# A decoder layer on one core: four modulation rows move into the Strassen pairs, and two small parts of the down projection change places

## The chip, the core and the metric

The kernel runs on one core of one Trainium2 chip. The core has five engines that run side by side: TensorE (PE, matrix products, with its weight loads shown apart as PEld), VectorE (DVE), ScalarE (ACT), GpSimd (POOL) and SyncE (SP, which here only issues transfers). They share an on-chip memory, TensorE writes its results into the accumulator banks PSUM, and 16 DMA engines move data from and to the main memory. ACT and POOL issue transfers too, each on a queue of its own. The metric is the device time of one execution in microseconds, from runs on the chip; lower is better.

## What is computed

One layer of a decoder: a mixer (an mLSTM head group and a convolution group) and a feed-forward part with a causal convolution, each between norms and scaled by a condition vector. The part that matters here is the modulation and the feed-forward:

```python
cond = jax.nn.silu(c)
mod = cond @ ada_w[l] + ada_b[l]
sh1, sc1, g1, sh2, sc2, g2 = jnp.split(mod[:, None, :], N_MOD, axis=-1)
...
u = rms_norm(x, ffn_pre_g[l]) * (1.0 + sc2) + sh2
up = causal_dwconv(u @ ffn_up[l], ffn_conv_w[l], ffn_conv_b[l])
a, gt = jnp.split(up, 2, axis=-1)
f = (jax.nn.silu(gt) * a) @ ffn_down[l]
x = x + g2 * rms_norm(f, ffn_post_g[l])
```

There are 512 positions, 1024 channels and 2816 feed-forward channels, all in float32. The last eighth of `mod` (48 blocks of 128 numbers), `g2`, is used only at the very end.

## The kernel before

**Numbers in two parts.** TensorE multiplies numbers of a shorter format. Each float32 operand z is therefore split into a high part `zh` (ACT copies it into the short format) and a low part `zl` = z - `zh`, and each product is made of three matmuls: high by high, high by low, low by high. The low part comes from VectorE (`split`), from GpSimd (`w_split`), or, in `added_split`, from a transfer: ACT writes -`zh` into `zl` and a DMA issued by POOL adds z to it (line 1088).

**The feed-forward up part.** The 2816 channels are 22 units of 128, each with a value half and a gate half. Units 0 to 7 are plain: two halves of 24 matmuls (512 wide), then `conv3` on ACT and VectorE (names `fa<i>c`, `fg<i>c`; two taps at line 999), a silu on ACT (line 1141) and a product on VectorE into a tile F (line 1142). Units 8 to 21 go in seven pairs, m = 4 to 10: the even unit i by a Strassen scheme of seven half-size products, the odd unit j plainly. TensorE's order in a pair is: four first products (p1, p7, p5, p6), the value half of j, three last products (p2, p3, p4), the gate half of j. The last products add onto banks that VectorE has to combine first (`between`, lines 1113 to 1116; line 1115 writes the bank `upx` that p2 goes on with). So line 1115 must be done when the value half is.

**The order around.** From the first pair on, ACT, VectorE and POOL run in the order in which the code is written (`in_order`); TensorE and SP always do. Before the pairs a scheduler orders ACT, VectorE and POOL, from its estimates and a few order marks.

**The modulation rows.** A row of `mod` is one 128 x 1024 tile of the weights, times the condition vector `cb`, summed on VectorE with one instruction (`ada_block`, line 155, followed by a short read of the accumulator). Rows 40 to 47 are `g2`. Rows 40 to 43 are summed just before the plain units' first results, rows 44 to 47 behind the results of units 4 and 5, marked to stand behind their line 1142. `ada_done` (line 160) and `gain` (line 667) finish them; `send_rows`, in pair m = 9, turns them and sends them to main memory, and in pair m = 10 ACT issues two transfers (line 663) that spread them over all partitions (`g2r`). Tiles `ada` come from a pool of two buffers, which pairs 9 and 10 use for other things.

**The down part.** It is Strassen again, over 11 blocks m of 256 channels. Its first half makes products with the forms b1, t1, t3, t2 of each weight block (`forms1`, `parts1`; b1 of blocks 0 to 4 by `part_b`, that is by `added_split`). The first product of all needs `b_0`, which is made in the last pair, m = 10, behind `g2r`'s transfers on ACT. The second half needs b2, b4 and t4 of each block and the parts of the tiles `g2kept`. `load2` brings for each block the quarter for b2, the quarter for b4 and the stored t2 (`t2_d`), from which `forms2` (line 1245) makes t4's source; `parts2` splits all three. VectorE's steps there carry order marks only ("order on VectorE"). Buffers `wd` and `wdmore` hold the loads, and each is used again for a later block, so a load waits until the splits of the earlier block have read it. At the end, the products of blocks 8 to 10 are taken apart by token blocks: first those with t4 (token blocks 2 and 3), then those with b2 and b4 (blocks 0 and 1), so that the final norm of each can start early. Each is followed on ACT and VectorE by a sum of squares, a factor and the addition of x, and by the transfer of the result.

Of the kernel before, what the change touches and what calls it, by code (L numbers as in the profile page):

```python
# [17 lines left out]
P = 128  # L18
# [34 lines left out]
def decoder_layer(ctx, tc, w_glu0, x, xT, c, adaT, vecs, w_glu, w_qko, w_v0, w_v, w_out, w_up, w_down, out):  # L53
# [1086 lines left out]
    def unit_out(i, a, g, F):  # L1140
        S.activation(g, g, AF.Silu)
        return V.tensor_tensor(out=F[:, (i % 2) * T : (i % 2 + 1) * T], in0=a, in1=g, op=ALU.mult)

# [84 lines left out]
    def load2(m):  # L1228
        r = wd_raw(m + NM, 2)
        loaded[m] = [quarter(r, b) for b in range(3)]  # L1230
        nc.sync.dma_start(r[:, :T], w_down[m][:, :T])
        nc.sync.dma_start(r[:, T : 2 * T], w_down[m][:, 3 * T :])
        nc.sync.dma_start(r[:, 2 * T : 3 * T], t2_d[m])

# [22 lines left out]
    for m in range(MS):  # L1257
        open_F(m)
        for i in (2 * m, 2 * m + 1):
            pa, pg = plain_unit(i)  # L1260
            if m < MS - 1:
                done = unit_out(i, conv3(pa, i, f"fa{i}"), conv3(pg, NF + i, f"fg{i}"), Fs[m])
                if i > 3:
                    for n in (2 * i + 36, 2 * i + 37):
                        ada_block(n, done)
                if i == 5:
                    ada_done(40, 48)
                    gain(3, 40, "ffn_post_g")
            elif i % 2 == 0:
                even = pa, pg  # L1270
            if i in (3, 4):
                token_forms(i - 3)
# [16 lines left out]
    with in_order():  # L1289
# [14 lines left out]
        for m in range(MS, NM):  # L1304
# [12 lines left out]
            bg = conv3(bg, NF + bj, f"fg{bj}")  # L1317
            weight_form(i, "p3", s4)
            if more_to_come:
                for n, q in ((i, 2), (i, 0), (j, 0), (i, 3), (j, 1), (i, 1)):  # L1320
                    up_load(n + 2, (q,))
# [24 lines left out]
            else:  # L1346
                part_b(0)
                part_b(1)
# [6 lines left out]
            if more_to_come:  # L1355
                weight_form(i + 2, "p7", a11)
                weight_form(i + 2, "p5", a21)
                value = [value_part(j + 2, 0)]
                V.tensor_tensor(out=a11, in0=a22, in1=a11, op=ALU.subtract)
            if m - 1 < SPILLED:  # L1360
# [7 lines left out]
            if more_to_come:  # L1368
                weight_form(i + 2, "p6", a11)
                value.append(value_part(j + 2, 1))  # L1370
            unit_out(i, vx, vz, Fs[m])
            before = j, va, pg
        more = upool.tile([P, 2, 2048], F32, tag="uh", name="wdmore")
# [87 lines left out]
    for m in range(NM):  # L1461
# [3 lines left out]
        if m > 1:  # L1465
            forms2(m)
            w2[m] = parts2(m)
        if M2 - NT <= m < M2:
# [139 lines left out]
```

## Time and profile before

| | |
|---|---|
| runs on the chip | 775.94, 772.1 and 770.09 us, median 772.1 |
| the profiled execution | 770.89 us, its span 769.2 us |
| TensorE clock granted | 0.999 |
| ACT busy | 449.0 us of the span (58%) |
| DMA | 148.47 MB, on the mean 193 GB/s |

The span runs from the first to the last instruction of the profiled execution; the time of that execution is 1.7 us longer. All moments below are microseconds from the span's start.

Busy time of the engines in stretches of 20 us (the last one 29) tells where in the program what is full:

```profile
440.00:460.00 20.00, 20.00 (x136) 18.54 (x135) 17.15 (x22) 11.71 (x20) 8.05 (x8) 1.00 0.86 223
...
500.00:520.00 20.00, 18.64 (x108) 16.15 (x108) 18.07 (x34) 14.15 (x26) 9.85 (x9) 1.00 0.77 196
...
580.00:600.00 20.00, 20.00 (x129) 18.27 (x128) 14.52 (x24) 13.53 (x25) 11.24 (x10) 1.00 0.74 174
...
640.00:660.00 20.00, 18.59 (x99) 15.79 (x98) 16.31 (x28) 12.23 (x23) 4.41 (x5) 1.00 0.94 267
...
720.00:740.00 20.00, 20.00 (x90) 16.57 (x89) 20.00 (x36) 13.75 (x28) 0.00 (x0) 1.00 0.86 291
740.00:769.00 29.00, 22.07 (x96) 17.58 (x95) 20.23 (x36) 10.20 (x24) 2.21 (x4) 0.97 0.44 162
```

Each row has the stretch, its length and then the busy time of TensorE, its weight loads, VectorE, ACT and GpSimd with the number of instructions, and last the granted clock, the share of time that the DMA engines were busy, and GB/s. The plain units run from about 440 to 506, the pairs from 506 to 655, the down part from there. TensorE is full nearly everywhere: it misses 1.4 us in the row of the first pair, 1.4 in the row in which the down part begins, and 6.9 in the last, which holds the final additions. VectorE is nearly full before the pairs, has some 5 us free in 20 within them, and is full again in the down part.

### The profile page before, as it was taken

The page shows a single profiled execution, that of the slowest core. Times are in us where ns is not written, and L with a number is a line of the kernel's source. Part 1 is how long each engine was busy: PE and PEld are TensorE (multiplying, and loading weights), DVE is VectorE, ACT ScalarE, POOL GpSimd, SP SyncE. Part 2 cuts the span into 40 slices and gives each one's busy share as a digit, 9 for nine tenths or more (in the row PEclk, how much of TensorE's full clock was granted, in tenths as well). Part 3 has the DMA queues.
Part 4 walks back from the last instruction along what each step waited for, and adds up shares of the span by engine and source line. Part 5 has one row for each costly group of instructions (what it writes and reads, how often), then busy time and mean ns, then how long its engine had stood idle before and what let it go on. Part 6 is the DMA issues. An engine that isn't in the chain of part 4 may idle for free.

```text
span 769.2 us, 11554 instructions
## 1 busy us (share of the span) xinstructions
PE 754.2 (98%) x3961; PEld 644.7 (84%) x3961; DVE 641.4 (83%) x1034; ACT 449.0 (58%) x860; POOL 367.6 (48%) x320
## 2 busy tenths in 40 slices
PE   7999999999999999999999999999999999999996
PEld 6888898778888888988888998878999989788884
DVE  6978999999999966756858789888877766999996
ACT  5457266776666447572353556677667656556752
POOL 1029587696798645442761444446665553100001
PEclk9999999999999999999999999999999999999999
DMA  9983214213022452425952788879877788799882
GB/s 331 380 291 137 84 55 164 82 51 143 29 90 102 161 172 106 165 109 182 373 202 109 248 221 220 247 191 275 202 179 174 177 239 202 219 338 373 288 301 109
DMA packets 55999, 148.47 MB, mean 193 GB/s; under 512 B 6370, under 2 KB 7810, under 8 KB 51844
## 3 DMA queue, kind: packets, MB, share of 16 engines
q1 hardware_dynamic: 33588, 100.37, 37.6%
q10 hardware_dynamic: 14288, 32.68, 12.1%
q0 software_dynamic: 8064, 14.68, 11.0%
q8 instruction: 31, 0.51, 0.3%
q14 instruction: 28, 0.23, 0.1%
HBM read 117.42 MB, written 15.61 MB: 173 GB/s over the span
## 4 chain that ended last, share of the span: by engine, by line
PE 59%; DVE 27%; DMA 5%; ACT 4%; issue 3%; ACTq 1%; POOL 0%; DVEq 0%; SPq 0%; POOLq 0%
DVE cv L731 10%; PE up L189 4%; PE up L190 4%; PE up L188 4%; PE upx L1095 4%; PE glu L316 3%; PE glu L189 3%; PE glu L190 3%; PE glu L188 3%; PE p L189 3%; PE p L190 3%; PE p L188 3%; PE mixa L188 2%; PE mixa L190 2%; PE mixa L189 2%
## 5 line engine op out<-in xcount | busy, mean ns | idle before, releaser
L731 DVE SCALAR_TENSOR_TENSOR cv<-gt,cvw,cv 128x505 f32<-128x505 f32 (+24 forms) x200 | 137.2, 729 | 2.3 <-ACT cv L719 1.1
L727 POOL TENSOR_TENSOR cs<-cs,cs 128x510 f32<-128x510 f32 (+3 forms) x32 | 41.8, 1305 | 0.3
L685 POOL TENSOR_TENSOR ro2r<-ro2t,mhalf 128x1 f32<-128x1 f32 x1 | 0.6, 559 | 81.3 <-DVE ro2t L683 81.3
L155 DVE SCALAR_TENSOR_TENSOR junk<-ada,cb 128x1024 bf16<-128x1024 f32 x20 | 31.2, 1562 | 7.9 <-DMA ada<-in_adaT 7.7
L725 ACT ACTIVATE cs<-gt,cvw 128x511 f32<-128x511 f32 (+4 forms) x40 | 27.4, 716 | 6.1 <-POOL cs L727 2.8
L188 PE MATMUL up<-u2h,wup_0h 128*128 128x512 f32 (+1 forms) x72 | 25.7, 357 | 0.2 <-DVE fa7c L999 0.2
L189 PE MATMUL up<-u2l,wup_0h 128*128 128x512 f32 (+1 forms) x72 | 25.7, 356 | 0.2 <-DVE u2l L910 0.2
L190 PE MATMUL up<-u2h,wup_0l 128*128 128x512 f32 (+1 forms) x72 | 25.5, 354 | 0.0
L171 POOL TENSOR_TENSOR wglu_0l<-wglu,wglu_0h 128x512 fp32r<-128x512 f32 x4 | 5.2, 1297 | 40.8 <-ACT wglu_0h L170 40.8
L171 POOL TENSOR_TENSOR wqko_1024l<-wqko,wqko_1024h 128x512 fp32r<-128x512 f32 x12 | 15.5, 1293 | 18.4 <-ACT wqko_1024h L170 13.0
L155 DVE SCALAR_TENSOR_TENSOR junk<-spare,cb 128x1024 bf16<-128x1024 f32 x12 | 19.0, 1584 | 3.1 <-DMA spare<-in_adaT 2.8
L188 PE MATMUL qko<-uh,wqko_1024h 128*128 128x512 f32 x48 | 20.6, 430 | 0.0
L188 PE MATMUL qko<-uh,wqko_0h 128*128 128x512 f32 x48 | 20.2, 420 | 0.0
L276 DVE SCALAR_TENSOR_TENSOR junk<-ada,cb 128x1024 bf16<-128x1024 f32 x16 | 19.5, 1219 | 0.1
L171 POOL TENSOR_TENSOR wo_512l<-wo,wo_512h 128x512 fp32r<-128x512 f32 x8 | 13.0, 1627 | 12.9 <-ACT wo_512h L170 12.9
L171 POOL TENSOR_TENSOR wqko_0l<-wqko,wqko_0h 128x512 fp32r<-128x512 f32 x12 | 16.7, 1388 | 5.0 <-ACT wqko_0h L170 5.0
L190 PE MATMUL qko<-uh,wqko_1024l 128*128 128x512 f32 x48 | 18.8, 392 | 0.0
L190 PE MATMUL qko<-uh,wqko_0l 128*128 128x512 f32 x48 | 18.8, 391 | 0.0
L171 POOL TENSOR_TENSOR wqko_512l<-wqko,wqko_512h 128x512 fp32r<-128x512 f32 x12 | 17.0, 1420 | 3.6 <-ACT wqko_512h L170 3.6
L189 PE MATMUL qko<-ul,wqko_1024h 128*128 128x512 f32 x48 | 18.7, 390 | 0.0
L189 PE MATMUL qko<-ul,wqko_0h 128*128 128x512 f32 x48 | 18.7, 390 | 0.0
L190 PE MATMUL qko<-uh,wqko_512l 128*128 128x512 f32 x48 | 18.7, 389 | 0.0
(1237 smaller groups left out, 3108.8 us busy)
## 6 DMA issues: line engine op xcount, KB each, us to landing
wups<-in_w_up SPq DMA_DIRECT2D x56, 256.0 KB, 4.7
wqko<-in_w_qko SPq DMA_DIRECT2D x12, 1024.0 KB, 4.8
ada<-in_adaT ACTq DMA_DIRECT2D x20, 512.0 KB, 4.1
ada<-in_adaT SPq DMA_DIRECT2D x16, 512.0 KB, 7.0
wo<-in_w_out SPq DMA_DIRECT2D x8, 1024.0 KB, 4.8
wup<-in_w_up SPq DMA_DIRECT2D x8, 1024.0 KB, 6.1
spare<-in_adaT ACTq DMA_DIRECT2D x12, 512.0 KB, 7.1
wd<-in_w_down SPq DMA_DIRECT2D x20, 256.0 KB, 5.9
```

The costliest lines, as they stand in the source:

```text
L155: t = V.scalar_tensor_tensor(out=junk, in0=r, scalar=1.0, in1=cb, op0=ALU.mult, op1=ALU.mult, accum_out=mod[:, i : i + 1])
L171: (eng or G).tensor_tensor(out=lo[:, :n], in0=src, in1=hi[:, :n].bitcast(F32), op=ALU.subtract)
L188: PE.matmul(ps, a[0], b[0], start=start, stop=False)
L189: PE.matmul(ps, a[0], b[1], start=False, stop=False)
L190: PE.matmul(ps, a[1], b[0], start=False, stop=stop)
L276: V.scalar_tensor_tensor(out=junk, in0=first[k][:, i * D : (i + 1) * D], scalar=1.0, in1=cb, op0=ALU.mult, op1=ALU.mult, accum_out=part[k] ...
L316: PE.matmul(banks0[i], blk(wk, i)[a], u[k][b], start=k == 0 and a == b, stop=False)
L685: G.tensor_tensor(out=r, in0=t, in1=mhalf[:, :1], op=ALU.pow)
L725: S.activation(t[:, d:], cvx[j][:, : T - d], AF.Copy, scale=w(CK - 1 - d))
L727: G.tensor_tensor(out=side[:, d:], in0=side[:, d:], in1=t[:, d:], op=ALU.add)
L731: last_tap[0] = V.scalar_tensor_tensor(out=cp[:, d:], in0=cvx[j][:, : T - d], scalar=w(CK - 1 - d), in1=cp[:, d:], op0=ALU.mult, op1=ALU.add)
L1095: PE.matmul(ps, x, y, start=start and k == 0 and n == 0, stop=stop and k == NT - 1 and n == 2, skip_group_check=True)
```

## The change

It has three parts.

1. Rows 44 to 47 leave the plain units. Each is loaded and summed in one of the pairs m = 5 to 8: the load on ACT's queue after the split of the next pair's first value quarter (`ada_fetch`), the sum on VectorE behind the pair's own result (`ada_add`). `ada_done` and `gain` follow in pair 8. With them go the order marks that tied the old sums to line 1142, and the scheduler orders the plain units' last operations anew.
2. In the last pair `part_b(0)` moves ahead: from behind `g2r`'s transfers to right behind the split of p3.
3. For blocks 8 to 10, `parts2` splits t4 first. And in every `load2` the stored t2 is fetched second, ahead of the quarter for b4.

```diff
     def unit_out(i, a, g, F):
         S.activation(g, g, AF.Silu)
-        return V.tensor_tensor(out=F[:, (i % 2) * T : (i % 2 + 1) * T], in0=a, in1=g, op=ALU.mult)
+        V.tensor_tensor(out=F[:, (i % 2) * T : (i % 2 + 1) * T], in0=a, in1=g, op=ALU.mult)
+
+    def ada_fetch(i):
+        r = adas.tile([P, D], F32, tag="ada", name=f"ada_{i}")
+        nc.scalar.dma_start(r, adaT[i // 2][:, (i % 2) * D : (i % 2 + 1) * D])
+        return r
+
+    def ada_add(i, r):
+        junk = small.tile([P, D], BF16, tag="junk", bufs=1, name=f"junk_{i}")
+        V.scalar_tensor_tensor(out=junk, in0=r, scalar=1.0, in1=cb, op0=ALU.mult, op1=ALU.mult, accum_out=mod[:, i : i + 1])
...
         nc.sync.dma_start(r[:, :T], w_down[m][:, :T])
+        nc.sync.dma_start(r[:, 2 * T : 3 * T], t2_d[m])
         nc.sync.dma_start(r[:, T : 2 * T], w_down[m][:, 3 * T :])
-        nc.sync.dma_start(r[:, 2 * T : 3 * T], t2_d[m])
...
             if m < MS - 1:
-                done = unit_out(i, conv3(pa, i, f"fa{i}"), conv3(pg, NF + i, f"fg{i}"), Fs[m])
-                if i > 3:
-                    for n in (2 * i + 36, 2 * i + 37):
-                        ada_block(n, done)
-                if i == 5:
-                    ada_done(40, 48)
-                    gain(3, 40, "ffn_post_g")
+                unit_out(i, conv3(pa, i, f"fa{i}"), conv3(pg, NF + i, f"fg{i}"), Fs[m])
...
             weight_form(i, "p3", s4)
+            if not more_to_come:
+                part_b(0)
...
             else:
-                part_b(0)
                 part_b(1)
...
                 value = [value_part(j + 2, 0)]
+                if MS < m < MS + 5:
+                    ada = ada_fetch(m + 39)
...
             unit_out(i, vx, vz, Fs[m])
+            if MS < m < MS + 5:
+                ada_add(m + 39, ada)
+            if m == MS + 4:
+                ada_done(40, 48)
+                gain(3, 40, "ffn_post_g")
...
-            w2[m] = parts2(m)
+            w2[m] = parts2(m) if m < M2 else parts2(m, 2, 3) | parts2(m, 0, 2)
```

What stands in a row on the engines, at three places. First VectorE at the end of unit 5, before the change; `junk` is the sum of a modulation row, `F` the unit's result, `ysum` the first step on it, `fa6c` the next unit:

```order
L999 SCALAR_TENSOR_TENSOR fg5c<-up_1_4910,vec,fg5c 128x510
L1142 TENSOR_TENSOR F_4744<-fa5c,fg5c 128x512
L155 SCALAR_TENSOR_TENSOR junk_4947,mod<-ada_4945,cb 128x1024
L1024 TENSOR_TENSOR ysum<-F_4744 128x256
L999 SCALAR_TENSOR_TENSOR fa6c<-up_0_4996,vec,fa6c 128x511
L155 SCALAR_TENSOR_TENSOR junk_4951,mod<-ada_4949,cb 128x1024
L1025 TENSOR_TENSOR F_4744<-F_4744 128x256
```

And after it, at the same place:

```order
L999 SCALAR_TENSOR_TENSOR fg5c<-up_1_4902,vec,fg5c 128x510
L1142 TENSOR_TENSOR F_4744<-fa5c,fg5c 128x512
L1024 TENSOR_TENSOR ysum<-F_4744 128x256
L1025 TENSOR_TENSOR F_4744<-F_4744 128x256
L1026 TENSOR_TENSOR ysum<-ysum,F_4744 128x256
```

The two sums are gone from here (two more from behind unit 4), and the steps on F follow each other. Second, ACT in the last pair before the change; `s_10` is the form of p3, `wup_2` a quarter of the gate:

```order
L170 ACTIVATE wup_p3h<-s_10_6722 128x512
L1141 ACTIVATE fg19c<-fg19c 128x512
L1086 ACTIVATE wup_2h<-wups_5119 128x512
L1087 ACTIVATE wup_2l<-wups_5119 128x512
...
L663 DMA g2r<-row_d_1362 128x512 x2
L1086 ACTIVATE b_0h<-wd_0_6528 128x512
L1087 ACTIVATE b_0l<-wd_0_6528 128x512
L1086 ACTIVATE b_1h<-wd_1_1_6691 128x512
```

After it:

```order
L170 ACTIVATE wup_p3h<-s_10_6722 128x512
L1086 ACTIVATE b_0h<-wd_0_6528 128x512
L1087 ACTIVATE b_0l<-wd_0_6528 128x512
L1141 ACTIVATE fg19c<-fg19c 128x512
L1086 ACTIVATE wup_2h<-wups_5101 128x512
```

The two splits of b_0 stand 12 rows sooner, and on POOL the adding transfer of b_0l stands ahead of those of wup_2l and wup_3l. Third, VectorE at the end of the down part before the change; `wd_20` and `wdmore` hold the loads of blocks 9 and 10, and the rows that write them in place make t4's source:

```order
L1245 TENSOR_TENSOR wd_20_7750<-wd_20_7750 128x512
L1016 TENSOR_TENSOR b_9l<-wd_20_7750,b_9h 128x512
L1245 TENSOR_TENSOR wdmore<-wdmore 128x512
L1016 TENSOR_TENSOR t_9l<-wd_20_7750,t_9h 128x512
L1016 TENSOR_TENSOR b_10l<-wdmore,b_10h 128x512 x2
L1016 TENSOR_TENSOR t_10l<-wdmore,t_10h 128x512
```

After it:

```order
L1254 TENSOR_TENSOR wd_20_7750<-wd_20_7750 128x512
L1016 TENSOR_TENSOR t_9l<-wd_20_7750,t_9h 128x512
L1016 TENSOR_TENSOR b_9l<-wd_20_7750,b_9h 128x512
L1254 TENSOR_TENSOR wdmore<-wdmore 128x512
L1016 TENSOR_TENSOR b_9l<-wd_20_7750,b_9h 128x512
L1016 TENSOR_TENSOR t_10l<-wdmore,t_10h 128x512
L1016 TENSOR_TENSOR b_10l<-wdmore,b_10h 128x512 x2
```

t_10l stands ahead of the two b_10l now. Earlier in the down part the only moves on VectorE are of three such in-place rows, each by one to three places; one of them, for `wd_16`, now stands ahead of t_2l instead of two rows behind it. TensorE's order is the same throughout.

## The prediction

> **What bounds the kernel now.** I read the page first, then the list of what TensorE waited for from 440 us on, then the timeline around each of those waits.
>
> ```profile
> PE 754.2 (98%) x3961; PEld 644.7 (84%) x3961; DVE 641.4 (83%) x1034; ACT 449.0 (58%) x860; POOL 367.6 (48%) x320
> ...
> PE p L189 <- DMA b_0l<-wd: 1.4, 1, 1.4
> PE upx L1095 <- DVE upx L1115: 1.1, 1, 1.1
> PE p L1454 <- DVE t_10l L1016: 0.4, 1, 0.4
> PE up L188 <- DVE fa7c L999: 0.2, 1, 0.2
> ```
>
> TensorE is busy 754.2 of 769.2 us, and the change leaves its matmuls and their order alone. So the change can win no more than TensorE's waits. All of them after 440 us are in the four rows, and each part of the change sits ahead of one: the first Strassen pair waits for VectorE (fa7c, then line 1115), the first down product waits for b_0l, and the last products wait for t_10l. The timeline of TensorE prices them from start to start:
>
> ```profile
> 511.58 0.28 PE L1095 MATMUL upw<-t2h,wup_p6l 128*128 128x256 f32 x1
> 512.10 0.47 PE L188 MATMUL up<-u2h,wup_0h 128*128 128x512 f32 x1 [0.24 <-DVE fa7c L999]
> ...
> 517.19 0.39 PE L189 MATMUL up<-u2l,wup_1h 128*128 128x512 f32 x1
> 517.41 0.39 PE L190 MATMUL up<-u2h,wup_1l 128*128 128x512 f32 x1
> 518.92 0.36 PE L1095 MATMUL upx<-u2h,wup_p2h 128*128 128x256 f32 x1 [1.12 <-DVE upx L1115]
> ...
> 655.15 0.39 PE L188 MATMUL p<-b_0h,fh 128*128 128x512 f32 x1
> 656.95 0.50 PE L189 MATMUL p<-b_0l,fh 128*128 128x512 f32 x1 [1.41 <-DMA b_0l<-wd]
> ...
> 750.70 0.39 PE L1454 MATMUL p<-t_10h,g2h 128*128 128x512 f32 x1
> 751.44 0.50 PE L1454 MATMUL p<-t_10l,g2h 128*128 128x512 f32 x1 [0.35 <-DVE t_10l L1016]
> ```
>
> A 512-wide matmul follows the last after about 0.23 us (517.19 to 517.41), a 256-wide one after 0.12 (561.26 to 561.38, quoted below). The losses are 0.52 - 0.12 = 0.40, 1.51 - 0.23 = 1.28, 1.80 - 0.23 = 1.57 and 0.74 - 0.23 = 0.51: 3.76 us in all.
>
> **Part one: four adds leave the plain units.**
>
> ```profile
> L155 DVE SCALAR_TENSOR_TENSOR junk<-ada,cb x4: 1210/1215/2592, 487.8 to 501.6; 128x1024 bf16<-128x1024 f32 x4
> 490.82 2.59 DVE L155 SCALAR_TENSOR_TENSOR junk<-ada,cb 128x1024 bf16<-128x1024 f32 x1
> 490.70 1.63 POOL L171 TENSOR_TENSOR wup_p1l<-wups,wup_p1h 128x512 fp32r<-128x512 f32 x1
> 518.35 0.42 DVE L1115 TENSOR_TENSOR upx<-upx,u 128x256 f32<-128x256 f32 x1
> ```
>
> VectorE loses 3 x 1.22 + 2.59 = 6.2 us between 487.8 and 502.8. It works there in program order and is behind TensorE: line 1115 ends at 518.77 and TensorE wanted it at 517.64. It has 1.1 us to make up and gets 6.2. What it may not pass is the end of the four first products (511.9, from the rows above), after which come two ACT copies and two additions of 0.4 us: about 514, still 3 us early. fa7c comes earlier by the same adds. I take both waits as gone, 0.40 + 1.28 = 1.68; the bounds are 0 and 1.68.
>
> **The same adds in pairs 5 to 8.** Each pair gets a 512 KB load on ACT's queue behind the wup_0 split, an add of 1.3 us with its accumulator read after the pair's own F, and in pair 8 two operations on 8 columns. Behind the add on VectorE stand s, the two taps of fg and then the steps up to line 1115; TensorE waits for that one.
>
> ```profile
> 543.16 0.62 ACT L1087 ACTIVATE wup_0l<-wups 128x512 fp32r<-128x512 f32 x1
> 549.37 0.69 DVE L1313 TENSOR_TENSOR s<-wups 128x512 f32<-128x512 f32 x1
> 551.06 1.53 DVE L999 SCALAR_TENSOR_TENSOR fg11c<-up,vec,fg11c 128x511 f32<-128x511 f32 x2 [1.00 <-ACT fg11c L997]
> 556.41 0.42 DVE L1113 TENSOR_TENSOR u<-upx,p 128x256 f32<-128x256 f32 x1 [0.28 <-ACT p L1112]
> 557.28 0.42 DVE L1115 TENSOR_TENSOR upx<-upx,u 128x256 f32<-128x256 f32 x1
> ...
> DMA to landing us min/median/max: 3.7/4.5/5.4
> ...
> 561.26 0.28 PE L1095 MATMUL upx<-u2h,wup_p2h 128*128 128x256 f32 x1
> 561.38 0.28 PE L1095 MATMUL upx<-u2l,wup_p2h 128*128 128x256 f32 x1
> ```
>
> Two waits for ACT (1.00 and 0.28) swallow 1.28 us, and line 1115 ends 3.56 us before TensorE needs it: 4.84 us of cover against 1.3. The load is issued at about 543.8; with the landings of such loads from 480 us on (the row in the middle) it is there from 547.5 to 549.2, ahead of the add's turn at 549.4. Cost: 0. If VectorE had no cover it would be 4 x 1.3 = 5.2, the upper bound. The issue itself takes ACT some 0.3 us, and s and with it p3 come 1.3 us later, needed only by TensorE's products after line 1115. An add can also meet GpSimd, as the rows at 490.70 and 490.82 show: it took 1.37 us longer than its 1.22 and was held until 492.2, when GpSimd's subtraction ended. In a pair that leaves 4.84 - 1.30 - 1.37 = 2.2 us of cover. The Trainium skill (SBUF — State Buffer, section on the two separate sides of SBUF) says that a GpSimd operation and a VectorE operation with two SBUF inputs take a shared port pair for the whole instruction while the other is blocked; by that rule the trace's 1.37 us is a full block, the sum stays 767.1, and rival one below is the likelier for it.
>
> **Part two: b_0 ahead of the gate's quarters in the last pair.**
>
> ```profile
> 639.35 0.63 ACT L1141 ACTIVATE fg19c<-fg19c 128x512 f32<-128x512 f32 x1 [1.14 <-DVE fg19c L999]
> 644.37 2.66 ACTq L663 DMA_DIRECT2D g2r<-row_d x2
> 647.08 0.63 ACT L1086 ACTIVATE b_0h<-wd 128x512 fp32r<-128x512 f32 x1 [3.42 <-DVE wd_0b L1185]
> 641.43 0.88 POOL L1088 DMA_DIRECT2D wup_2l<-wups x1 [0.54 <-ACT p L1111]
> wup_2l<-wups POOLq DMA_DIRECT2D x1, 256.0 KB, 5.7
> b_0l<-wd POOLq DMA_DIRECT2D x1, 256.0 KB, 8.0
> 656.72 1.52 DVE L999 SCALAR_TENSOR_TENSOR fg20c<-upz,vec,fg20c 128x511 f32<-128x511 f32 x2
> ```
>
> b_0's two splits stand behind 2.66 us of row DMAs on ACT (644.37 to 647.03; the releaser named in the brackets was done earlier); they move into a hole of 1.14 us ahead of the silu of fg19c. b_0l's accumulating DMA then goes out at about 641 instead of 648.9, and even 8.0 us later it has landed long before 655.4. The wait of 1.57 goes. What is behind it: wup_2l and wup_3l go out one issue (0.9 us) later, so wup_2l lands at 648.0; TensorE's gate half begins 24 x 0.227 before 655.15, at 649.7. Next, p7's bank must be read out by fg20c, which ends at 658.24; TensorE would want it 12 matmuls after 655.15, at 657.87. But ACT is rid of two splits (0.63 us each, overlapping a little) ahead of fa21c, and VectorE, which waits for fa21c there, starts about 1 us earlier. I take the full 1.57; the bounds are 0 and 1.57, and 1.2 if fg20c does not move.
>
> **Part three: t4 first at the end, t2 second in each load.**
>
> ```profile
> 724.57 0.33 SPq L1232 DMA_DIRECT2D wdmore<-in_w_down x1
> 726.71 0.33 SPq L1233 DMA_DIRECT2D wdmore<-t2d x1
> 725.99 0.69 DVE L1016 TENSOR_TENSOR t_2l<-wdmore,t_2h 128x512 fp32r<-128x512 f32 x1
> 727.80 0.39 PE L1454 MATMUL p<-t_2l,g2h 128*128 128x512 f32 x1
> 748.28 0.69 DVE L1245 TENSOR_TENSOR wdmore<-wdmore 128x512 f32<-128x512 f32 x1 [1.42 <-DMA wdmore<-t2d]
> 749.49 1.29 DVE L1016 TENSOR_TENSOR b_10l<-wdmore,b_10h 128x512 fp32r<-128x512 f32 x2
> ```
>
> At the end t_10l no longer stands behind the two b_10l (1.29 us). The form that it comes from ends at 748.97, one ACT split (0.63) follows, so t_10l starts at about 749.8 instead of 750.70 and ends at 750.5; TensorE wants it at 750.93. The 0.51 goes, with 0.4 us to spare. b_10l is needed only some 18 matmuls (4 us) later. Against it stands SP's queue: where the buffer's old t part is freed last, t2 now waits at 726.71 and holds b4, which went out at 724.57. That puts the queue back by one issue, 0.4 us, about what t2 gains by going out one transfer sooner (256 KB at the 400 GB/s of the row under rival two, some 0.65 us): net 0. The order also puts wd_16's subtraction (0.6 us) ahead of t_2l, which then ends at 727.3, before TensorE's 727.80. Cost 0; bounds -0.5 and +0.5.
>
> **Sum.** 1.68 + 0 + 1.57 + 0.51 = 3.76. The profiled execution took 770.89 us (span 769.2): 770.9 - 3.8 = 767.1. The median of the three runs, 772.1, is 1.2 above that execution and the runs spread from 770.09 to 775.94, so the range leans up.
>
> **Rivals.**
> *One, slower: the adds' loads come late.* ACT issues them amid other traffic. An add may wait 3.5 us in a pair before TensorE stands, a landing after 9.1 us; every further us costs four. From landings of 10 us on the gain is eaten; at 12 us the time is 767.1 + 4 x 2.9 = 778.7. Against it: no ada load of that stretch took over 5.4. Chance 5%.
>
> *Two, the end takes it back.* TensorE reaches the end 3.3 us sooner, but the last loads come no sooner, since DMA is at its limit:
>
> ```profile
> GB/s 405 406 396 351 234 382 410 399 404 387 314 65 184 304 335 133 265 355 274 280 403 337 398 400 394 393 347 51 0 0 0 0 304 78 226 61 243 0 272 32
> ```
>
> These are 40 slices of 700 to 769 us. About 400 GB/s from 734 on speaks for it; the holes at 65, 184 and 133 speak against it, for there the queue waits for VectorE to free buffers, and VectorE comes earlier with TensorE. If nothing moves, only 0.5 is won: 770.4. Chance 13%.
>
> *Three, b_0l's wait is only replaced* by wup_2l or p7's bank: 767.1 + 1.57 = 768.7 at most. Chance 14%.
>
> *Four, the change does nothing* because VectorE is late in the first pair for another reason: 1.68 less, 768.8. Chance 4%.
>
> **Chances.** The forecast has 64%, between 765.6 and 768.6. One per cent, about what a measurement of this kernel can tell from no change, is 7.7 us; all waits together are half of that. Faster by over 1% only by the runs' spread: 0.05. Slower by over 1% needs rival one with landings past 12 us: 0.03. Within: 0.92. The range leaves out most of rival one and the lucky end: 764.8 to 771.3.
>
> **What would show it.** After: no TensorE wait for line 1115, fa7c, b_0l or t_10l; line 1115 in pairs 6 to 9 about 0.1 to 1.5 us nearer to TensorE's need but ahead of it; b_0h at about 638; the pairs 21.0 us apart as before. Wrong it is if TensorE waits for line 1115 in a later pair, if VectorE waits for ada for over 3 us, or if p or up in the down part waits for a DMA that is not in the rows above.

## The result, and the profile after

The changed kernel takes 768.08 us (median of 8 runs, 766.66 to 769.81), the kernel before 772.51 on the same chip (8 runs, 770.09 to 775.94): a ratio of 0.9943, with an interval from 0.9923 to 0.9964. A second comparison, later, gave 768.75 against 772.03: 0.9963 (0.9949 to 0.9977). So the change wins 0.2 to 0.8%, within the one per cent that was forecast as most likely. The profiled execution took 769.46 us, with a span of 767.7.

The page after, and the list of what TensorE waited for from 440 us to the end:

```profile
PE 753.0 (98%) x3961; PEld 644.1 (84%) x3961; DVE 640.2 (83%) x1034; ACT 449.9 (59%) x860; POOL 367.2 (48%) x320
```
```profile
PE up L190 <- DMA wup_2l<-wups: 0.4, 1, 0.4
PE p L1465 <- DVE t_10l L1016: 0.2, 1, 0.2
```

The waits for line 1115, fa7c and b_0l are no longer in the list. t_10l still is, and wup_2l has come in. The timeline of TensorE prices them from start to start, as the prediction did:

```profile
649.47 0.40 PE L189 MATMUL up<-u2l,wup_2h 128*128 128x512 f32 x1
650.26 0.50 PE L190 MATMUL up<-u2h,wup_2l 128*128 128x512 f32 x1 [0.40 <-DMA wup_2l<-wups]
650.60 0.40 PE L188 MATMUL up<-u2h,wup_2h 128*128 128x512 f32 x1
...
749.29 0.49 PE L1465 MATMUL p<-t_10h,g2h 128*128 128x512 f32 x1
750.02 0.50 PE L1465 MATMUL p<-t_10l,g2h 128*128 128x512 f32 x1 [0.23 <-DVE t_10l L1016]
```

wup_2l costs 0.79 - 0.23 = 0.56, and 0.11 more because the matmul after a wait starts late as well (650.26 to 650.60). t_10l costs 0.73 - 0.23 = 0.50, the 0.51 of before. Reckoned so from 440 us on, with the small gaps behind each wait, TensorE lost 4.50 us before and 1.42 after: 3.08 less. The medians differ by 4.4; the part of the program ahead of 440 us, which the change leaves alone, varies by over 1 us between executions (the first 512-wide matmul of the plain units starts at 451.52 us in the profile before and at 453.17 in this one), so the experiments are read by TensorE's losses first.

The new sums in the pairs, the first of them on VectorE, and TensorE where it needs line 1115 (groups of the tile ada from 530 to 660 us, then the timelines of VectorE and TensorE):

```profile
L1146 ACTq DMA_DIRECT2D ada<-in_adaT x4: 339/340/340, 540.6 to 603.9; - x4
L1151 DVE SCALAR_TENSOR_TENSOR junk<-ada,cb x4: 1218/1218/1220, 548.7 to 611.7; 128x1024 bf16<-128x1024 f32 x4
...
DMA to landing us min/median/max: 3.8/4.3/4.7
```
```profile
548.75 1.22 DVE L1151 SCALAR_TENSOR_TENSOR junk<-ada,cb 128x1024 bf16<-128x1024 f32 x1
549.89 0.69 DVE L1316 TENSOR_TENSOR s<-wups 128x512 f32<-128x512 f32 x1
...
555.97 0.43 DVE L1113 TENSOR_TENSOR u<-upx,p 128x256 f32<-128x256 f32 x1 [0.45 <-ACT p L1112]
...
556.84 0.42 DVE L1115 TENSOR_TENSOR upx<-upx,u 128x256 f32<-128x256 f32 x1
```
```profile
560.82 0.28 PE L1095 MATMUL upx<-u2h,wup_p2h 128*128 128x256 f32 x1
```

All four sums take 1.22 us, no load is late, and line 1115 ends at 557.26, 3.56 us ahead of TensorE: exactly the lead of before. The two waits for ACT (1.00 and 0.28 before) have shrunk to one of 0.45. Behind the next two sums the lead is 3.56 as well. Behind the fourth it is 2.19, where it was 3.59 before, because `ada_done` (line 160) follows that sum, 8 columns wide, and ends together with GpSimd's subtraction:

```profile
613.01 2.02 DVE L160 TENSOR_TENSOR mod<-mod,vec 128x8 f32<-128x8 f32 x1
```
```profile
613.37 1.62 POOL L171 TENSOR_TENSOR wup_p4l<-wups,wup_p4h 128x512 fp32r<-128x512 f32 x1
```

It takes 2.00 to 2.02 us in all eight profiles that have it there with single sums, and 0.15 to 0.17 in the others. TensorE does not wait for it.

In the last pair, b_0's splits have moved into the hole, and b_0l's transfer stands ahead of wup_2l's on GpSimd's queue (timelines of ACT and of GpSimd, then the landings):

```profile
637.67 0.62 ACT L1086 ACTIVATE b_0h<-wd 128x512 fp32r<-128x512 f32 x1
```
```profile
640.09 1.22 POOL L1088 DMA_DIRECT2D b_0l<-wd  x1
641.23 0.98 POOL L1088 DMA_DIRECT2D wup_2l<-wups  x1
```
```profile
wup_2l<-wups POOLq DMA_DIRECT2D x1, 256.0 KB, 9.0
```

641.23 + 9.0 = 650.23, where TensorE wanted it at 649.70. At the end, SP's queue around block 6 and the form of block 10:

```profile
720.97 0.33 SPq L1240 DMA_DIRECT2D wdmore<-in_w_down  x1
725.85 0.33 SPq L1241 DMA_DIRECT2D wdmore<-t2d  x1
726.23 0.42 SPq L1242 DMA_DIRECT2D wdmore<-in_w_down  x1
...
741.48 0.32 SPq L1241 DMA_DIRECT2D wdmore<-t2d  x1
742.11 0.33 SPq L1242 DMA_DIRECT2D wdmore<-in_w_down  x1
```
```profile
747.79 0.69 DVE L1254 TENSOR_TENSOR wdmore<-wdmore 128x512 f32<-128x512 f32 x1 [0.59 <-DMA wdmore<-t2d]
```

The form came 0.49 us sooner than before (748.28), TensorE 1.41 sooner (t_10h at 749.29 against 750.70). t_10l stands ahead of b_10l as planned and is late all the same.

### The profile page after: what moved, and what is told of

Read it like the earlier page. It is cut to its first block, busy times and chain, and to the rows that moved or that the text cites. A ratio compares the mean times of both kernels' runs of the same rounds, so it can differ in the third digit from the quotient of the medians.

```text
span 767.7 us, 11547 instructions
## 1 busy us (share of the span) xinstructions
PE 753.0 (98%) x3961; PEld 644.1 (84%) x3961; DVE 640.2 (83%) x1034; ACT 449.9 (59%) x860; POOL 367.2 (48%) x320
## 4 chain that ended last, share of the span: by engine, by line
PE 67%; DVE 22%; DMA 6%; ACT 2%; issue 2%; POOL 1%; ACTq 0%; DVEq 0%; POOLq 0%; SPq 0%
DVE cv L731 10%; PE up L190 7%; PE up L189 7%; PE up L188 7%; PE upx L1095 4%; PE glu L189 3%; PE glu L190 3%; PE glu L188 3%; PE p L1465 3%; PE p L189 3%; PE p L188 3%; PE p L190 3%; PE upz L1095 2%; PE mixa L188 2%; PE mixa L190 2%
## 5 line engine op out<-in xcount | busy, mean ns | idle before, releaser
L155 DVE SCALAR_TENSOR_TENSOR junk<-ada,cb 128x1024 bf16<-128x1024 f32 x16 | 24.9, 1559 | 7.2 <-DMA ada<-in_adaT 7.0
L276 DVE SCALAR_TENSOR_TENSOR junk<-ada,cb 128x1024 bf16<-128x1024 f32 x16 | 19.5, 1220 | 0.1
L171 POOL TENSOR_TENSOR wo_1024l<-wo,wo_1024h 128x512 fp32r<-128x512 f32 x8 | 11.7, 1456 | 14.9 <-ACT wo_1024h L170 14.9
```

Of the source, the lines that this page charges most:

```text
L155: t = V.scalar_tensor_tensor(out=junk, in0=r, scalar=1.0, in1=cb, op0=ALU.mult, op1=ALU.mult, accum_out=mod[:, i : i + 1])
L171: (eng or G).tensor_tensor(out=lo[:, :n], in0=src, in1=hi[:, :n].bitcast(F32), op=ALU.subtract)
L276: V.scalar_tensor_tensor(out=junk, in0=first[k][:, i * D : (i + 1) * D], scalar=1.0, in1=cb, op0=ALU.mult, op1=ALU.mult, accum_out=part[k] ...
```

## Experiments

The table has what TensorE lost from 440 us on, in us, by what it waited for (with the gap behind each wait; the total holds small ones too; in the column of wup, the 0.27, 0.54, 0.34 and 0.11 of the four kernels with waits in the first pair are wup_2l's of that pair, the others belong to the last pair), and the ratio of the times to the kernel before. The kernels follow in order.

| kernel | fa7c and line 1115 | wup_0l, wup_2l | b_0l | t2 to t_10 | total | ratio (interval) |
|---|---|---|---|---|---|---|
| before | 1.82 | 0.27 | 1.68 | 0.62 | 4.50 | 1 |
| changed | 0 | 0.67 | 0 | 0.65 | 1.42 | 0.9943 (0.9923 to 0.9964) |
| adds alone | 0 | 0 | 0 | 0.75 | 0.84 | 0.9961 (0.9945 to 0.9978) |
| adds alone, again | 0 | 0 | 0 | 2.01 | 2.10 | 0.9960 (0.9946 to 0.9974) |
| b_0 alone | 1.54 | 0.54 | 0 | 0.73 | 2.91 | 0.9980 (0.9968 to 0.9992) |
| end alone | 2.56 | 0 | 0.60 | 1.20 | 4.48 | 0.9989 (0.9977 to 1.0002) |
| adds twice | 2.23 | 0.34 | 0.76 | 0.39 | 3.83 | 1.0001 (0.9986 to 1.0017) |
| b_0l's transfer behind | 0 | 0 | 0 | 0.93 | 1.02 | 0.9958 (0.9941 to 0.9975) |
| t2 third | 0 | 0.47 | 0 | 0 | 0.56 | 0.9955 (0.9939 to 0.9970) |
| t2 second late | 0 | 0.28 | 0 | 0.19 | 0.56 | 0.9942 (0.9928 to 0.9955) |
| adds and t4 first | 0 | 0 | 0 | 0.31 | 0.40 | 0.9948 (0.9932 to 0.9964) |
| changed, again | 0 | 0 | 0 | 0.74 | 0.83 | 0.9963 (0.9949 to 0.9977) |
| before, again | 3.18 | 0.11 | 2.05 | 0.61 | 6.05 | 0.9994 (0.9976 to 1.0013) |

**Part one alone, and once more.** Against the changed kernel:

```diff
-            if not more_to_come:
-                part_b(0)
...
             else:
+                part_b(0)
                 part_b(1)
...
-            w2[m] = parts2(m) if m < M2 else parts2(m, 2, 3) | parts2(m, 0, 2)
+            w2[m] = parts2(m)
```
(and t2 third again in each load)

> Part one alone: the four modulation sums are in the pairs, the order of b_0 and of the end is that of before. Theory (the adds alone made VectorE late in the first pair): TensorE's waits for fa7c and for line 1115 go (0.40 + 1.28 us, and up to 0.4 more of small ones beside them), b_0l's wait of 1.57 and t_10l's of 0.51 stay, and no new wait stands in pairs 6 to 9; the time is 1.7 to 2.1 us below before. Rival (the new adds cost in the pairs): line 1115 shows a wait for VectorE in pairs 6 to 9, and the gain is under 1 us. Rival (VectorE is late in the first pair for another reason): line 1115's wait stays at over 1 us.

> The kernel with part one alone once more, since b_0l was there in time in it without part two: ACT's two row transfers took 1.48 us to issue there, 2.66 in the profile before. Theory (the length of these issues is chance from execution to execution, and b_0l is late where they are long): with a new execution they take another time between 1.4 and 3.1 us, and b_0l's issue moves by that; TensorE waits for it where they take over 2.3. Rival (part one itself brings them forward, by the transfers that it takes out of the plain units): 1.5 us again within 0.2, no wait for b_0l.

The first pair's waits went, and no pair has a new one. But b_0l's wait, which was to stay, went too, in both executions. The timelines of ACT and GpSimd and the landing, of the first of them:

```profile
642.66 1.48 ACTq L663 DMA_DIRECT2D g2r<-row_d  x2
644.19 0.63 ACT L1086 ACTIVATE b_0h<-wd 128x512 fp32r<-128x512 f32 x1 [1.58 <-DVE upz L1116]
```
```profile
645.99 0.87 POOL L1088 DMA_DIRECT2D b_0l<-wd  x1 [2.90 <-ACT b_0l L1087]
```
```profile
b_0l<-wd POOLq DMA_DIRECT2D x1, 256.0 KB, 6.5
```

b_0 stands behind the row transfers as before, but they took 1.48 us to issue in place of 2.66, and the transfer landed after 6.5 us in place of 8.0: at 652.5, well before TensorE wanted it. The second execution has 1.44 and 6.5. So it is not chance of one execution, as the theory for the second run had it. There t_9l and t_10l were late by 0.79 and 1.00 (plus 0.11 each): the end varies by over 1 us with the landing of its last loads.

**Part two alone.** Against the kernel before:

```diff
             weight_form(i, "p3", s4)
+            if not more_to_come:
+                part_b(0)
...
-                part_b(0)
                 part_b(1)
```

> Part two alone: b_0 a pair's half sooner, everything else as before. Theory (wup_2l queues behind b_0l on GpSimd's own queue): b_0l's wait of 1.57 goes, wup_2l lands some 9 us after its issue where it took 5.7 before, and TensorE waits 0.5 to 0.8 us for it about 5 us earlier in the program; the waits of the first pair and of t_10l stay; the time is 0.8 to 1.1 us below before. Rival (the new wait for wup_2l in the changed kernel came of TensorE being 2 us earlier, not of the queue): wup_2l lands after 6 us or so and is not waited for, and the whole 1.57 is won.

b_0l's whole wait of 1.68 went and wup_2l was not waited for in the last pair, although it landed after 7.8 us. Half of the theory holds (the landing), half of the rival (it is not missed where TensorE comes later): lateness here hangs on some tenths. The median is 1.1 us below that of before.

**Part three alone.** Against the kernel before:

```diff
+        nc.sync.dma_start(r[:, 2 * T : 3 * T], t2_d[m])
         nc.sync.dma_start(r[:, T : 2 * T], w_down[m][:, 3 * T :])
-        nc.sync.dma_start(r[:, 2 * T : 3 * T], t2_d[m])
...
-            w2[m] = parts2(m)
+            w2[m] = parts2(m) if m < M2 else parts2(m, 2, 3) | parts2(m, 0, 2)
```

> Part three alone: t4 first for the last three blocks, t2 second in each load, everything else as before. Theory (the end is set by the loads, and the new order moves only what stands behind the form): the form of block 10 ends within 0.5 us of where it ended before against TensorE, and t_10l, no longer behind b_10l, is in time or late by under 0.3 us; 0.3 to 0.5 us are won. Rival (the load in second place costs as much as the order wins): t_10l's wait stays at 0.4 us or more and nothing is won. The waits for fa7c, line 1115 and b_0l stay as they were (0.40, 1.28, 1.57).

The rival holds: t_10l's 0.50 is there in full, and t_2l and b_3l have waits of 0.14 and 0.05 that were not there before. b_0l, whose code is that of before, was late by 0.49 this time and not 1.57, with a landing of 7.0 us.

**The adds twice: why was b_0l in time with part one?** The kernel before, with part one's loads and sums done over again in the pairs:

```diff
+                if MS < m < MS + 5:
+                    ada = ada_fetch(m + 39)
...
+            if MS < m < MS + 5:
+                ada_add(m + 39, ada)
```

> The kernel before, whole, with the loads and sums of part one done over again in the pairs (into a place that nothing reads), so the plain units stay as they were. It asks why b_0l was in time with part one alone and late by 0.5 to 1.9 us without. Theory (the adds in the pairs hold s and the taps behind them 1.3 us longer, weight buffers come free later, and SP's loads of the down weights move back by 1.2 to 1.9 us, away from b_0l's transfer): the waits of the first pair stay (0.4 to 1.8 for fa7c, 1.28 for line 1115), b_0l lands after 5.5 to 6.5 us in place of 7.0 to 8.6, and TensorE does not wait for it; about 1.5 us below before. Rival (TensorE's own waits in the first pair set how it stands to the loads): b_0l is late as before, the time that of before or 0.5 above it.

The rival holds: b_0l is late by 0.65, with a landing of 7.2 us. The sums in the pairs are not what brings it in time; taking the four out of the plain units is. The same run shows that these sums cost nothing in the pairs: no wait there, ratio 1.0001. For the seven profiles with b_0 in its old place, in us and from the silu of fg18c, after which TensorE wants b_0l by 20.55 us in each:

| kernel | first pair's waits | next wd load on SP | ACT's three issues | b_0l issued | landed after | late by |
|---|---|---|---|---|---|---|
| before | 1.82 | 6.05 | 3.79 | 14.04 | 8.0 | 1.57 |
| before, again | 3.18 | 6.07 | 3.61 | 13.87 | 8.6 | 1.94 |
| end alone | 2.56 | 6.06 | 3.74 | 14.00 | 7.0 | 0.49 |
| adds twice | 2.23 | 6.06 | 3.70 | 13.94 | 7.2 | 0.65 |
| adds alone | 0 | 7.27 | 1.88 | 12.19 | 6.5 | - |
| adds alone, again | 0 | 7.18 | 1.83 | 12.14 | 6.5 | - |
| adds and t4 first | 0 | 6.57 | 3.61 | 13.91 | 5.5 | - |

Without the first pair's waits TensorE and ACT are ahead by those 1.8 to 3.2 us there, and SP's loads, which move up by less, fall 0.5 to 1.2 us later against them. In all three such profiles b_0l's transfer is faster, in two its issue is earlier too. That the loads' traffic is what slows it fits this table, but no run moved the loads alone, so this stays open.

There is another side to it at wup_0l, earlier in the last pair (all profiles but that of the five sums, below). SP's six loads of down weights begin 4.6 to 4.9 us ahead of wup_0l's issue in the five profiles with waits in the first pair, and it lands after 4.1 to 4.9 us. In the eight without those waits (single sums) they begin 2.3 to 3.3 us ahead of it, and it lands after 7.1 to 9.4 us, where TensorE wants it 9.1 us after its issue. So with part one b_0l's transfer is faster and wup_0l's slower, up to the edge of a wait. Here too no run moved the loads alone.

**b_0l's transfer behind wup_2l and wup_3l.** The changed kernel with b_0's splits where it has them and the transfer later on GpSimd's queue:

```diff
             if not more_to_come:
-                part_b(0)
+                part_b_splits(0)
...
             if not more_to_come:
+                part_b_add(0)
```

> The changed kernel, with b_0's two splits as early as it has them but its accumulating transfer issued on GpSimd's queue behind those of wup_2l and wup_3l. Theory (wup_2l lands late because b_0l's transfer stands ahead of it in that queue): wup_2l lands after about 6 us as before the change, TensorE's wait for it (0.56 + 0.11 us) goes, b_0l is issued at about 643.5 and lands by 652 to 653, before TensorE wants it at about 655; no new wait: 0.6 to 0.7 us below the changed kernel. Rival (the transfers of that stretch are slow because of all the other traffic, whatever their order): wup_2l still lands after 8 us or more and the wait stays. Second rival (the wait is only passed on): wup_2l is in time, and b_0l or the bank of p7 is waited for by a like amount.

In its last pair (landings from 634 to 656 us):

```profile
wup_2l<-wups POOLq DMA_DIRECT2D x1, 256.0 KB, 6.5
...
b_0l<-wd POOLq DMA_DIRECT2D x1, 256.0 KB, 8.7
```

wup_2l landed after 6.5 us and was in time; b_0l, issued at 644.36, landed at 653.06, 2.8 us ahead of TensorE. The queue's order decides: in "t2 second late", which has the same order on this queue, wup_2l landed after 3.9 us. But 0.33 us of the gain came back as a wait for t_10h at the end, and the total is 0.4 below that of the changed kernel; the times (0.9958) can't tell them apart.

**t2 third again, t4 first kept.** Against the changed kernel:

```diff
-        nc.sync.dma_start(r[:, 2 * T : 3 * T], t2_d[m])
         nc.sync.dma_start(r[:, T : 2 * T], w_down[m][:, 3 * T :])
+        nc.sync.dma_start(r[:, 2 * T : 3 * T], t2_d[m])
```

> The changed kernel with t2 third in each load, as before the change; t4 first for the last three blocks is kept. Theory (t2's hold of SP's queue and its earlier place cancel, as the prediction had it): the form of block 10 and t_10l stand within 0.3 us of the changed kernel against TensorE, the wait for t_10h and t_10l together is 0.4 to 0.9 us, the same time. Rival one (second place is worth a transfer): the form comes 0.6 us or more later, and TensorE waits 1.0 to 1.3 us. Rival two (the hold costs more than the place wins): the queue runs on some 1.5 us earlier at block 6, the form is in time, and the wait goes: 0.5 us below the changed kernel.

Rival two holds: nothing is left of the waits at the end. SP's queue at the same places, and the form:

```profile
720.10 0.33 SPq L1240 DMA_DIRECT2D wdmore<-in_w_down  x1
722.84 0.33 SPq L1241 DMA_DIRECT2D wdmore<-in_w_down  x1
724.98 0.33 SPq L1242 DMA_DIRECT2D wdmore<-t2d  x1
...
740.99 0.33 SPq L1242 DMA_DIRECT2D wdmore<-t2d  x1
```
```profile
746.41 0.69 DVE L1254 TENSOR_TENSOR wdmore<-wdmore 128x512 f32<-128x512 f32 x1 [0.30 <-DMA wdmore<-t2d]
```

TensorE stands where it stood in the changed kernel (in the pair before the last, it takes up line 1115's result at 623.80 against 623.84). The list of what SP waited for shows how the buffer of block 6 comes free in two steps; with t2 third (first fence) each transfer waits for its own, with t2 second (the changed kernel, second fence) one waits for both and b4 stands behind it:

```profile
SPq L1241 <- DVE s L1016: 3.0, 2, 2.7
SPq L1242 <- DVE s L1016: 2.1, 1, 2.1
```
```profile
SPq L1241 <- DVE s L1016: 4.8, 1, 4.8
```

So b4 of block 6 goes out 3.4 us sooner with t2 third (722.84 against 726.23), the queue's last issue is 1.1 us sooner (740.99 against 742.11), and t2 of block 10 goes out 0.49 us sooner from third place than from second. The form is 1.38 us sooner.

What the queue lost is not the wait of b4. Behind block 6 it stands 1.25 us later with t2 second (726.23 against 724.98). Of this, 0.38 is the one issue that stands behind t2, and 0.26 is TensorE, which lost more in the last pair (it starts the down part at 655.40 against 655.14). The other 0.61 comes from VectorE: with t2 second the in-place row for wd_16 stands ahead of t_2l, whose read frees the buffer (the changed kernel first, then t2 third):

```profile
724.53 0.69 DVE L1254 TENSOR_TENSOR wd<-wd 128x512 f32<-128x512 f32 x1
725.14 0.69 DVE L1016 TENSOR_TENSOR t_2l<-wdmore,t_2h 128x512 fp32r<-128x512 f32 x1
```
```profile
724.27 0.68 DVE L1016 TENSOR_TENSOR t_2l<-wdmore,t_2h 128x512 fp32r<-128x512 f32 x1
```

The four profiles with single sums and t2 second throughout have the row ahead of t_2l, the nine with t2 third in block 6 have it behind. wup_0l was late by 0.36 in the last pair of this execution, with a landing of 9.4 us (see the end of the section on the adds twice).

**t2 second for blocks 8 to 10 only**, on the kernel with b_0l's transfer behind:

```diff
+        b4 = lambda: nc.sync.dma_start(r[:, T : 2 * T], w_down[m][:, 3 * T :])
+        if m < M2:
+            b4()
         nc.sync.dma_start(r[:, 2 * T : 3 * T], t2_d[m])
-        nc.sync.dma_start(r[:, T : 2 * T], w_down[m][:, 3 * T :])
+        if m >= M2:
+            b4()
```

> The kernel of b0's transfer behind wup_3l, with t2 in second place only for blocks 8 to 10 and third for the blocks before them. Theory (only the last block's place counts, and in blocks before 8 the second place holds the queue): no hold of 1.5 us at block 6, t2 of block 10 still goes out ahead of b4, the form of block 10 is 0.4 us or more earlier against TensorE than with t2 second throughout, and of the waits for t_10h and t_10l, 0.83 us there, under 0.4 is left; in the last pair no wait. Rival (the end is set by the sum of the loads, not by their order): 0.6 us or more of wait stays.

As expected: 0.19 left at the end. But t2 third throughout left nothing, so second place shows no gain late either. The place on the queue is there (0.63 us in the changed kernel, 741.48 against 742.11), but the form of block 10 starts 6.3 us after t2's issue on the mean of the six profiles with t2 second in that block (5.9 to 6.5) and 5.9 us after it on the mean of the eight with t2 third (5.2 to 6.8). From that point (623.84 in the changed kernel) to the form of block 10, less the waits for b_0l and wup in between, the four profiles with t2 second throughout and single sums have 123.3 to 123.9 us, and those with it third 122.1 to 122.9 except one (123.7, the second execution of the adds alone).

**Five sums in place of one.** The changed kernel, each sum in the pairs repeated:

```diff
-    def ada_add(i, r):
+    def ada_add(i, r, again=4):
+        if again:
+            ada_add(i, r, again - 1)
```

> The changed kernel with each of the four sums in the pairs done five times over (the last one is the one that counts), so 6.1 us in place of 1.2 and 4.9 more in each of these pairs. Theory (the pair's cover of 4.84 us, from two waits for ACT of 1.28 and 3.56 in front of TensorE): line 1115 of the next pair starts later by the excess alone, TensorE waits 1.0 to 1.8 us for it in each of the four pairs, 4 to 7 us in all over the changed kernel. Rival one (no cover: VectorE bounds the pairs): the full 4.9 us in each, some 20 us over the changed kernel. Rival two (more cover than I counted): no wait for line 1115, under 1 us in all.

787.70 us, a ratio of 1.0213 (1.0195 to 1.0230): some 19 us over the changed kernel, near the sum of rival one, but the pairs do have cover. VectorE and GpSimd in the first of the four pairs with sums, TensorE at the end of that round, and the clock (columns: us, busy time of PE, PEld, DVE, ACT and POOL, granted clock, DMA share, GB/s):

```profile
548.01 1.22 DVE L1153 SCALAR_TENSOR_TENSOR junk<-ada,cb 128x1024 bf16<-128x1024 f32 x1
...
549.27 3.06 DVE L1153 SCALAR_TENSOR_TENSOR junk<-ada,cb 128x1024 bf16<-128x1024 f32 x1
...
556.07 0.69 DVE L1318 TENSOR_TENSOR s<-wups 128x512 f32<-128x512 f32 x1
```
```profile
549.64 1.61 POOL L171 TENSOR_TENSOR wup_p4l<-wups,wup_p4h 128x512 fp32r<-128x512 f32 x1
```
```profile
559.86 0.39 PE L190 MATMUL up<-u2h,wup_1l 128*128 128x512 f32 x1
562.71 0.35 PE L1095 MATMUL upx<-u2h,wup_p2h 128*128 128x256 f32 x1 [2.47 <-ACT fh L1032]
```
```profile
562.70:566.70 4.00, 3.99 (x21) 4.00 (x22) 3.97 (x6) 1.81 (x4) 2.00 (x3) 0.57 1.06 259
588.60:592.60 4.00, 3.99 (x33) 4.00 (x34) 3.96 (x6) 1.79 (x4) 1.99 (x3) 1.00 1.05 261
```

One sum of the five meets GpSimd's subtraction in every pair and takes 3.06 to 3.10 us, so five take 8.06 us (548.01 to 556.07) and not 6.1. The first stall is 2.62 us: s comes 8.06 - 1.14 = 6.92 later than in the changed kernel, less the cover left there (3.56 + 0.45) makes 2.9. So far the reckoning of the cover holds. (The profile names ACT's fh as the releaser, which ended at 562.58. But line 1115 ended at 562.56, and TensorE goes on 0.15 us behind line 1115 here as in the kernel before, 518.77 to 518.92.)

But the lead of 3.56 is spent by then and does not come back: the stalls of the next pairs are 3.3, 4.8 and 3.6 us. Line 1115 now comes at 562.14, 588.04 and 613.94, every 25.9 us, so VectorE's own round is 25.9 - 8.06 = 17.8 us without sums, and 21.0 - 17.8 leaves 3.2 us a pair for good. From here on VectorE bounds the pairs, as rival one has it. That each costs 25.9 - 21.0 = 4.9 us, rival one's figure, is chance: it is 8.06 less a cover of 3.2.

After the first, third and fourth stall the granted clock is 0.57, 0.52 and 0.64 for some 4 us, and 256-wide matmuls follow one another after 0.21 us in place of 0.12, some 1.6 us in all each time. Only the last of these adds to the time. The other two come out of the stall that follows, since line 1115 comes every 25.9 us with or without them: that stall is 3.3 and 3.6 us behind a slow stretch, and 4.8 behind a full clock. So the 19 us are 2.6 in the first pair, some 5 in each of three more and 1.5 behind the last stall.

**Only what earns.** Part one and t4 first; b_0 and t2 where they were before the change. Against the changed kernel:

```diff
-        nc.sync.dma_start(r[:, 2 * T : 3 * T], t2_d[m])
         nc.sync.dma_start(r[:, T : 2 * T], w_down[m][:, 3 * T :])
+        nc.sync.dma_start(r[:, 2 * T : 3 * T], t2_d[m])
...
-            if not more_to_come:
-                part_b(0)
...
             else:
+                part_b(0)
                 part_b(1)
```

> Part one and t4 first for the last three blocks; b_0 where it was before the change and t2 third in each load. Theory (of the change only these two parts earn anything once they stand together: b_0l is in time by part one, t2's second place costs): after the first plain units no TensorE wait over 0.3 us, b_0l and wup_2l in time, the form of block 10 and t_10l in time or late by under 0.2; 0.5 to 1.2 us below the changed kernel in the trace from the first pair on. Rival (b_0l needs part two after all): a wait for b_0l of 0.5 us or more. Second rival (t4 first without t2 second leaves t_10l late): a wait of 0.4 us or more there.

Beside it, the changed kernel and the kernel before once more, as they are:

> The changed kernel once more, to see which of its waits come again. If they belong to the program: wup_2l late by 0.5 to 0.8 us with a landing of 9 us, t_10l late by 0.4 to 0.7, t2 of block 6 issued some 5 us behind the transfer ahead of it. If they were chance of one execution, they move by half a us or more or are gone.

> The kernel before the change once more. If b_0l's wait belongs to the program: ACT's two row transfers take 2.4 us or more to issue, b_0l is issued some 12 us after the silu of fg18c and waited for, by 0.4 to 1.7 us (0.49 and 1.57 so far, by its landing of 7 or 8 us). If it was chance: they take 1.5 to 2 us, as with part one alone, and there is no wait. The waits for fa7c and line 1115 come again (0.3 to 1.1, and 1.28).

The smaller change has the smallest loss of all, 0.40 us, with b_0l and wup_2l in time and t_10l late by 0.20. Its median is 767.44 beside 768.75 of the changed kernel in the same comparison; the intervals overlap (0.9932 to 0.9964, 0.9949 to 0.9977), so it is better by the trace, and not shown to be by the time. In the changed kernel's second execution t_10l's 0.50 came again and the hold at block 6 too; wup_2l landed after 7.9 us and was not waited for, by 0.6 us. In the kernel before, b_0l's wait came again (1.94), as did line 1115's (1.27) and fa7c's (1.75).

## Why the prediction was right, and which terms failed

The time was forecast at 767.1 and came at 768.08, the gain at 3.8 and came at 3.1 by TensorE's losses in the first two profiles (5.2 in the second two, 6.05 against 0.83). That it came so near is in part luck. Against the terms of the sum, part one brought 0.41 more, part two 0.56 less with what it cost at wup_2l, and part three 0.54 less. And 767.1 counts from a profiled execution that lies 1.6 us below the median of the kernel before; from that median the same 3.76 gives 768.75.

- **Part one, 1.68.** Right, and a little small: with the gaps behind the waits and around wup_2l it was 2.09 in the profiled execution. The adds alone take both waits out, twice; adds in both places leave them. VectorE's late sums were the cause; their order marks left with them, and the two were not tried apart.
- **The same adds in the pairs, 0.** Right: no wait for line 1115 in any of these pairs, in any profile with single sums. The loads went out at 540.59, 3 us sooner than taken, and landed in 3.8 to 4.7 us against the 3.7 to 5.4 taken. The cover was mis-stated as one number for every pair: a first pair took up 5.4 us of sums (8.06 - 2.62, against 4.84), but each of a row of pairs can take only 3.2. One sum and a collision of 1.84 (3.06 - 1.22, against the 1.37 taken) would be 3.1, so it still fits, with 0.1 to spare rather than 2.2. The single sums escaped that collision by 0.4 us (the first ended at 549.97, GpSimd's subtraction began at 550.38). It met `ada_done` in pair 8 instead, an operation that the prediction named without a price, and took 1.4 us of the lead there. The Trainium skill (SBUF — State Buffer, section on the two separate sides of SBUF) has VectorE blocked for the whole of a GpSimd operation; the long sum agrees within 0.2 us: it took 1.84 more than its 1.22, and the subtraction beside it 1.61.
- **Part two, 1.57.** The wait went, but this was not part two's gain. The step took the four losses as independent; b_0l's wait was there only behind the first pair's (four profiles with them, late in all; three without, in time in all). On top of part one, part two wins nothing that these profiles show, and in one of the changed kernel's two it cost 0.67.
- **wup_2l one issue later, lands at 648.0.** This step failed: it moved the issue by 0.9 us and kept the landing of 5.7. The issue moved by 0.25 against the silu of fg18c (6.60 to 6.85 us behind it), the landing by 3.3. Behind b_0l on the queue it took 9.0, and 7.1 to 7.9 in four other profiles; without b_0l ahead it took 3.9 to 6.8 in nine. Rival three named this place, with its bound of 768.7, and it came for 0.67 of 1.57.
- **Part three, 0.51 with the queue at net 0.** This step failed. t4 first does its part: with t2 third, t_10l's loss fell to 0 and 0.20. The hold of the queue behind t2 is one issue, 0.38, as taken. What was missed is the row for wd_16: the prediction saw that it moves t_2l back by 0.6 and held this against TensorE alone, at no cost, but SP waits for t_2l as well, and its queue went back by the same 0.61. Against both stands the place won, 0.63, of which a slower landing takes 0.4 on the mean. Between the two profiles, the last issue comes 1.12 later, less 0.63 for the place, and the landing takes 0.89 more: the form is 1.38 later (0.26 of it TensorE's). Why a landing from second place is slower was not tried. Here rival two came true in small: the form moved up 0.49 where TensorE moved 1.41.

## What to carry to other kernels

Losses along one chain are not to be summed as if each stood alone: the first one sets how the later work stands to the loads, and taking it out may take a later one with it, or bring one in. A lead in front of the bottleneck is spent once, while a wait that repeats in every turn can be filled in every turn; cover for work added to a loop is the second only. Moving a transfer ahead on a queue can cost the one behind it far more than the issue: here 0.25 us of issue and 1.4 to 3.3 of landing. And where a new order moves a row on one engine, everything that waits for the rows behind it has to be priced, the queues that wait for a buffer too.

## What the runs showed of the hardware

- ACT issued the first of the pairs' loads at 540.59, while the two splits that stand ahead of it in the program began at 541.74 and 542.26: this transfer, which waits for nothing, goes out ahead of ACT's computing rows. The other three of the changed kernel do so too.
- Issuing the same three row and g2d transfers took ACT between 1.5 us (0.39 + 1.07, the changed kernel again) and 4.0 us (0.93 + 3.06, b_0l's transfer behind). What makes them long was not settled.
- VectorE's line 160 on the 8 columns of g2 took 2.0 us beside a subtraction of GpSimd (1.62 us), and 0.15 to 0.17 us in the six profiles where no such subtraction ran beside it.
- The granted clock fell after a stall of 2.6 us and not after the next, of 3.3 us (the two rows with the clock, under the five sums). The Trainium skill (TensorE: Matmul & The Clock Gate, part 1 on the clock gate) has the clock halved after an idle window of about 3.4 us that runs freely. That not every stall is hit agrees with a freely running window; that 2.6 us is enough does not agree with a whole idle window, and here the measurement decides.
